# Half of the low parts of two weight streams on GpSimd, and eleven single-pass weight units made three-pass

## The chip, the cores and the metric

The kernel runs on one core of a Trainium2 chip. A core has TensorE (matrix products, PE in the profile; PEld is its weight load), VectorE (DVE), ScalarE (ACT), GpSimd (POOL) and SyncE (SP, which here issues the DMAs). Each engine works through its own list of instructions in order. The metric is the device time of one execution in microseconds (us), and a time for a kernel is a median over runs. A change of about 0.2% (some 5.7 us) is the least that a measurement of this kernel can tell from none.

## The reference, cut to what matters

The network has two layers. Each layer mixes 256 context and 512 latent tokens of width 1024 through four branches, merges the branches, applies one output projection, then a post-norm (layer norm of a scaled residual plus the projection) and a gated MLP with a down projection and a second post-norm:

```
        out_lat = merge(px[0], (ret[1], mla[1], lru[1], ssd[1]))      # ... acc @ w_out
        new_lat = post_norm(h_lat, mod_x[2] * o_lat, ln1_w[l], ln1_b[l])
        f_lat = conv_ffn(modulate(new_lat, mod_x[3], mod_x[4]), ffn_w_up[l], ffn_conv_w[l], ffn_conv_b[l], ffn_w_down[l])
        new_lat = post_norm(new_lat, mod_x[5] * f_lat, ln2_w[l], ln2_b[l])
...
def conv_ffn(h, w_up, conv_w, conv_b, w_down):
    u = centred_conv(h @ w_up, conv_w, conv_b)
    g, v = u[..., :D_FF], u[..., D_FF:]
    return (jax.nn.silu(g) * v) @ w_down
```

The change touches `acc @ w_out` (1024 x 1024) and `(...) @ w_down` (2816 x 1024).

## The kernel before, in words

**Split products.** Most products are made of three matmuls in a 32-bit format of reduced precision (fp32r). An operand x is split into a high part, x rounded to fp32r, and a low part, x minus the high part. The product is then high x high + low x high + high x low, summed in PSUM. `split` (L215 to 217) does this for activations: a cast on ScalarE (L216) and a subtraction on VectorE (`tt`, L143). `unit` (L201 to 213) does it for a weight unit of 128 x 1024: a DMA into a raw tile `wr` (L198, on SP), a cast into `wh` on ScalarE (L205), and two subtractions of 128 x 512 into `wl` on VectorE (called at L209, shown at the helper's line L143). There are three raw tiles (`N_WR`), five high and five low ones.

**Plain products.** `PLAIN` (L55) names units of the output projection that are not split: for those `plain_unit` only loads the raw weights, `plain_pair` hands on the unsplit activations, and `prod` (L513 to 523) issues one fp32 matmul at L519, which the hardware runs as two passes, each with a record of its own. Eleven units are plain: all eight of the context pair in layer 0, and units 3, 5 and 7 of the second latent pair in layer 1.

**The two projections.** The tokens stand in pairs of 128-token tiles: pair 0 is context, pairs 1 and 2 are latents. The output projection works pair by pair in the order 1, 2, 0 (layer 1: 1, 2 alone), with 8 units per pair; the down projection does the same with 22 units per pair. For a unit `tm_wide` (L508) multiplies the pair's two tiles with both halves of the unit: 4 products of 512 columns, into four PSUM tiles `g`. `pair_of` splits the pair's activations for the unit (tiles `t`).

**Post-norm.** After each pair VectorE reads the four PSUM tiles (`o<-g`), adds the residual, takes statistics (`st`, `mv`, `rs`), and GpSimd raises `rs` to the power -1/2 (`rpow`, L190). In the output projection this is done twice. ScalarE normalises (L421), TensorE transposes the pair (L400), and ScalarE and VectorE write the pair into the transposed input `hT2` of the MLP as high and low parts (`hh`, `hl`). The first MLP units (`begin_up`, matmuls at L1518 to 1520) follow the last pair in program order; in layer 0 they need `hT2` of pairs 1 and 2, in layer 1 of pair 1 first.

**Order.** The program is written once; a scheduler of the language turns it into one list per engine by its own costs and by priorities (`tc.high_priority`: weight units and splits ahead of most other work). Those lists are fixed in the program, and an instruction waits for its inputs and buffers in its place in the list. The DMA issues of SP are in one list as well.

Of the kernel before, what the change touches and what calls it, by code (L numbers as in the profile page):

```python
# [8 lines left out]
F32 = mybir.dt.float32  # L9
# [15 lines left out]
NF = D_FF // P  # L25
# [26 lines left out]

N_EARLY = (6, 6)

PLAIN = {(0, 0): (0, 1, 2, 3, 4, 5, 6, 7), (1, 2): (3, 5, 7)}  # L55

STAG = ((0, 2), (0, 0), (3, 5))

# [40 lines left out]
def trunk(tc, xin, cc, const, pv, pr, rows, ada_b, ada_w, w_in, w_uq, w_ukv, w_lg, w_br, w_out, w_up, w_dn, out):  # L99
# [3 lines left out]
    def nm(p):  # L103
        uid[0] += 1
        return f"{p}{uid[0]}"
# [3 lines left out]
    with ExitStack() as ctx:  # L109
# [12 lines left out]
        act, dve, pool, pe, sy = nc.scalar, nc.vector, nc.gpsimd, nc.tensor, nc.sync  # L122
# [4 lines left out]
        def G():  # L127
            return pg.tile([P, 512], F32, tag="g", name=nm("g"))
# [7 lines left out]
        def T256(dt=F32, tag="t"):  # L136
            return tp.tile([P, 256], dt, tag=tag, name=nm("t"), bufs=N_T if tag == "t" else N_V)
# [4 lines left out]
        def tt(o, a, b, op):  # L142
            dve.tensor_tensor(out=o, in0=a, in1=b, op=op)  # L143
# [10 lines left out]
        MUL, ADD, SUB, MAX, MIN = ALU.mult, ALU.add, ALU.subtract, ALU.max, ALU.min  # L154
# [38 lines left out]
        def W4(tag, n, dt=F32R):  # L193
            return wp.tile([P, 1024], dt, tag=tag, name=nm(tag), bufs=n)

        def whole(ap, f=1024, tag="wr"):
            t = W4(tag, {"wr": N_WR, "wh": N_WH, "wl": N_WL}[tag], F32)
            sy.dma_start(out=t[:, 0:f], in_=ap[:, 0:f])  # L198
            return t

        def unit(ap, f=1024, shape=None):  # L201
            with tc.high_priority(offset=O_UNIT):
                raw = whole(ap, f)
                hi = W4("wh", N_WH)
                act.copy(hi[:, 0:f], raw[:, 0:f])  # L205
                lo = W4("wl", N_WL)
                for c in range(0, f, 512):
                    e = min(f, c + 512)
                    tt(lo[:, c:e], raw[:, c:e], hi[:, c:e].bitcast(F32), SUB)  # L209
            if shape is None:  # L210
                return hi, lo
            a, b = shape
            return (hi[:, 0:f].rearrange("p (a b) -> p a b", a=a), lo[:, 0:f].rearrange("p (a b) -> p a b", a=a))

        def split(src, hi, lo):  # L215
            act.copy(hi, src)  # L216
            tt(lo, src, hi.bitcast(F32), SUB)
# [172 lines left out]
        def to_hT(l, which, pair, xh, hT, kps=(0, 1, 2, 3)):  # L390

            strm = 1 if pair == 0 else 0
            t0 = 2 * pair * P
            mc = modc[l]
            for kp in kps:
                ps = C().rearrange("p (k a b) -> p k a b", k=2, a=2)
                for k2 in range(2):
                    k = 2 * kp + k2
                    for a in range(2):
                        pe.transpose(ps[:, k2, a, :], xh[a][k // 4][:, (k % 4) * P:(k % 4 + 1) * P], ident)  # L400
                for k2 in range(2):
                    k = 2 * kp + k2
                    tmp = T256()
                    pk = ps[:, k2, :, :].rearrange("p a b -> p (a b)")
                    if k2:
                        ts(tmp, pk, mc[:, 2 * which + 1, strm, k:k + 1], MUL, mc[:, 2 * which, strm, k:k + 1], ADD)
                    else:
                        act.activation(out=tmp, in_=pk, func=AF.Identity, bias=mc[:, 2 * which, strm, k:k + 1], scale=mc[:, 2 * which + 1, strm, k:k + 1])
                    split(tmp, hT[k][0][:, t0:t0 + 256], hT[k][1][:, t0:t0 + 256])
# [15 lines left out]
        def load_gate(l, which, s):  # L425

            bc = {}
            for h in range(2):
                bc["g", s, h] = S(w=512)
                sy.dma_start(out=bc["g", s, h], in_=modr[l][which, s, h:h + 1, :].to_broadcast([P, 512]))  # L430
            return bc
# [11 lines left out]
        def load_res(pair, res):  # L443

            rs = {}
            for a in range(2):
                for h in range(2):
                    r = rs[a, h] = S(w=512)
                    sy.dma_start(out=r, in_=res[2 * pair + a][:, 512 * h:512 * (h + 1)])
            return rs  # L450
# [44 lines left out]
        def pair_of(t, p, spare=False):  # L495

            with tc.high_priority(offset=100):
                if spare:
                    hi, lo = (hp.tile([P, T], F32R, tag="h", name=nm("h"))[:, 0:256] for _ in range(2))
                else:  # L500
                    hi, lo = T256(F32R, "v"), T256(F32R, "v")
                split(t[:, 2 * p * P:(2 * p + 2) * P], hi, lo)
            return [(hi[:, a * P:(a + 1) * P], lo[:, a * P:(a + 1) * P]) for a in range(2)]

        def plain_pair(t, p):
            return [(t[:, (2 * p + a) * P:(2 * p + a + 1) * P], None) for a in range(2)]

        def plain_unit(ap):  # L508
            with tc.high_priority(offset=100):
                return whole(ap), None  # L510

        def tm_wide(units, nk, xsl, last=0):

            ps = [[G(), G()] for _ in range(2)]

            def prod(k, wh, wl, x, a, h):
                xh, xl = x[a]
                cs = slice(512 * h, 512 * (h + 1))
                pe.matmul(ps[a][h], lhsT=xh, rhs=wh[:, cs], start=k == 0, stop=wl is None and k == nk - 1)  # L519
                if wl is None:  # L520
                    return
                pe.matmul(ps[a][h], lhsT=xl, rhs=wh[:, cs], start=False, stop=False)  # L522
                pe.matmul(ps[a][h], lhsT=xh, rhs=wl[:, cs], start=False, stop=k == nk - 1)  # L523

            held = []
            for k in range(nk):
                held.append((k, *units(k), xsl(k)))
                if k < nk - last:
                    for a in range(2):
                        for h in range(2):  # L530
                            prod(*held[0], a, h)
                    held.clear()
            for a in range(2):
                for h in range(2):
                    for i in held:
                        prod(*i, a, h)
            return ps
# [912 lines left out]
        for l in range(DEPTH):  # L1450
            full = l < DEPTH - 1
            pairs = (1, 2, 0) if full else (1, 2)
# [12 lines left out]
            acc = []  # L1465
# [56 lines left out]
            def begin_up():  # L1522

                for u in range(N_EARLY[l]):
                    ps = early[u] = G() if u < 4 else C()
                    up_part(u, ps, 0, CTX, SEQ if full else 256, True)

            for p in pairs:
                if p == 0:
                    bc.update(load_gate(l, 0, 1))  # L1530
                for a in range(2):
                    mid[2 * p + a] = dp.tile([P, D], F32, name=nm("mid"))
                rs = load_res(p, res)
                plain = PLAIN.get((l, p), ())
                ps = tm_wide(lambda k: plain_unit(w_out[l, k]) if k in plain else unit(w_out[l, k]), 8, lambda k: plain_pair(acc[k], p) if k in plain else pair_of(acc[k], p), STAG[0][l])
                xs = post_norm(p, ps, rs, bc, mid, True, PW[0][l])
                if p == pairs[-1]:
                    begin_up()
                with tc.high_priority(offset=LATER[1]):
                    to_hT(l, 1, p, xs, hT2)  # L1540
# [5 lines left out]
            sv = [None] * NF  # L1546
# [39 lines left out]
            for p in pairs:  # L1586
                if p == 0:
                    bc.update(load_gate(l, 1, 1))
                for a in range(2):
                    t = 2 * p + a  # L1590
                    new[t] = dp.tile([P, D], F32, name=nm("new")) if full else out[(t - 2) * P:(t - 1) * P, :]

                rs = load_res(p, mid)
                ps = tm_wide(lambda k: unit(w_dn[l, k]), NF, lambda k: pair_of(sv[k], p, not full and p == pairs[-1]), STAG[1 if p != pairs[-1] else 2][l])
                xs = post_norm(p, ps, rs, bc, new, full, PW[1 + (p == pairs[-1])][l])
                if full:
                    with tc.high_priority(offset=-LATER[0]):
                        to_hT(l + 1, 0, p, xs, hT)
# [158 lines left out]
```

## Time and profile before

| | us |
|---|---|
| median of 3 runs (lowest, highest) | 2859.02 (2856.67, 2859.52) |
| the profiled execution, and its span | 2861.12, 2859.3 |
| PE busy, of the span | 2801.5 (98%) |
| DVE busy | 1873.3 (66%) |
| ACT busy | 1246.2 (44%) |
| POOL busy | 54.0 (2%) |

Busy shares are averages over the span. A matmul record is longer than the distance to the next one, since matmuls are pipelined: what a matmul costs is read from one start to the next. The same holds for VectorE, where a 128 x 512 instruction is recorded with 0.68 us and the next one starts 0.60 us later. A bracket at a row's end gives the idle time before the instruction and what ended it.

### The profile page before, as it was taken

What the parts mean: (1) busy time and instruction counts of PE and PEld (TensorE: products, weight loads), DVE (VectorE), ACT (ScalarE), POOL (GpSimd) and SP (SyncE); (2) the same over time, 40 slices, a digit from 0 to 9 for tenths busy, and PEclk for the clock granted to TensorE, in tenths of its full rate; (3) what the DMA queues carried; (4) which work ended last, traced back from release to release, by engine and by line L of the source; (5) the groups of instructions that cost most, each with busy time, mean ns of one, the idle gap of its engine ahead of it and who ended that gap; (6) DMA issues with size and microseconds to landing.
All of it is one profiled execution on the core that took longest, in us unless ns stands there. A gap on an engine that the chain in (4) does not pass through costs nothing.

```text
span 2859.3 us, 40144 instructions
## 1 busy us (share of the span) xinstructions
PE 2801.5 (98%) x15248; PEld 2362.5 (83%) x15248; DVE 1873.3 (66%) x3933; ACT 1246.2 (44%) x2231; POOL 54.0 (2%) x70
## 2 busy tenths in 40 slices
PE   7999999999999999999999999999999999899998
PEld 5988879888888886888888778888888888688887
DVE  6454438767566448855557886545887785876667
ACT  4323235434455325533335653244554673453353
POOL 0000000000000001000000000000000000000000
PEclk9999999999999999999999999999999999999999
DMA  6212441445343345311125563121134234542265
GB/s 256 69 49 89 168 155 38 149 169 192 120 169 119 105 155 193 131 65 61 66 85 198 185 203 114 50 98 60 46 112 136 103 114 152 190 152 96 96 201 175
DMA packets 129170, 363.65 MB, mean 127 GB/s; under 512 B 14369, under 2 KB 29601, under 8 KB 128977
## 3 DMA queue, kind: packets, MB, share of 16 engines
q1 hardware_dynamic: 128976, 361.09, 37.0%
q8 instruction: 120, 1.97, 0.3%
q14 instruction: 74, 0.60, 0.1%
HBM read 332.59 MB, written 26.35 MB: 126 GB/s over the span
## 4 chain that ended last, share of the span: by engine, by line
PE 83%; DVE 8%; DMA 4%; ACT 2%; issue 1%; POOL 1%; SPq 0%; POOLq 0%; DVEq 0%; ACTq 0%
PE g L220 18%; PE g L221 18%; PE g L222 18%; PE g L519 3%; PE g L522 3%; PE g L523 3%; PE g L282 2%; PE g L283 2%; PE g L284 2%; DVE wl L143 2%; DVE o L143 1%; DMA wr<-in_w_dn_dram 1%; PE g L349 1%; DVE st L382 1%; PE g L252 1%
## 5 line engine op out<-in xcount | busy, mean ns | idle before, releaser
L143 DVE TENSOR_TENSOR wl<-wr,wh 128x512 fp32r<-128x512 f32 (+1 forms) x866 | 567.0, 682 | 436.1 <-ACT wh L205 402.0
L220 PE MATMUL g<-hh,wh 128*128 128x512 f32 (+1 forms) x2384 | 842.4, 353 | 0.8 <-DVE s L152 0.8
L221 PE MATMUL g<-hl,wh 128*128 128x512 f32 (+1 forms) x2384 | 837.5, 351 | 0.0
L222 PE MATMUL g<-hh,wl 128*128 128x512 f32 (+1 forms) x2384 | 837.0, 351 | 0.0
L205 ACT CAST wh<-wr 128x1024 fp32r<-128x1024 f32 x405 | 423.0, 1046 | 517.9 <-PE g L221 300.6
L220 PEld LDWEIGHTS g<-hh,wh 128*128 128x128 f32 x2384 | 451.2, 189 | 66.2 <-issue 6.6
L222 PEld LDWEIGHTS g<-hh,wl 128*128 128x128 f32 x2384 | 450.8, 189 | 58.5
L221 PEld LDWEIGHTS g<-hl,wh 128*128 128x128 f32 x2384 | 451.2, 189 | 57.4
L143 DVE TENSOR_TENSOR s<-s,s 128x256 f32<-128x256 f32 (+4 forms) x332 | 207.0, 645 | 26.3 <-ACT s L1121 14.6
L519 PE MATMUL g<-wh,t 128*128 128x512 f32 x468 | 184.2, 396 | 3.1 <-ACT t L216 2.5
L522 PE MATMUL g<-wh,t 128*128 128x512 f32 x468 | 183.1, 393 | 1.4 <-DVE t L143 1.3
L523 PE MATMUL g<-wl,t 128*128 128x512 f32 x468 | 182.2, 392 | 0.7 <-DVE wl L143 0.3
L221 PE MATMUL g<-s,wh 128*128 128x512 f32 (+1 forms) x452 | 160.6, 355 | 0.0
L220 PE MATMUL g<-s,wh 128*128 128x512 f32 (+1 forms) x452 | 160.2, 354 | 0.0
L222 PE MATMUL g<-s,wl 128*128 128x512 f32 (+1 forms) x452 | 159.8, 354 | 0.0
L152 DVE SCALAR_TENSOR_TENSOR s<-g,pv,s 128x511 f32<-128x511 f32 (+2 forms) x176 | 111.7, 643 | 61.3 <-ACT s L543 59.4
L152 DVE SCALAR_TENSOR_TENSOR s<-s,s 128x512 f32<-128x512 f32 (+2 forms) x130 | 98.2, 756 | 54.8 <-ACT s L1568 27.4
L152 DVE SCALAR_TENSOR_TENSOR s<-s,g 128x512 f32<-128x512 f32 x118 | 70.7, 604 | 90.8 <-PE g L222 57.3
L282 PE MATMUL g<-wh,hh 128*128 128x512 f32 (+1 forms) x320 | 124.5, 390 | 1.0 <-ACT s L662 1.0
L283 PE MATMUL g<-wh,hl 128*128 128x512 f32 (+1 forms) x320 | 124.3, 388 | 0.0
L284 PE MATMUL g<-wl,hh 128*128 128x512 f32 (+1 forms) x320 | 123.4, 386 | 0.0
L152 DVE SCALAR_TENSOR_TENSOR s<-g,fcg,s 128x511 f32<-128x511 f32 (+1 forms) x128 | 83.9, 655 | 52.0 <-ACT s L543 50.1
(297 smaller groups left out, 4357.9 us busy)
## 6 DMA issues: line engine op xcount, KB each, us to landing
wr<-in_w_in_dram SPq DMA_DIRECT2D x120, 512.0 KB, 3.5
wr<-in_w_dn_dram SPq DMA_DIRECT2D x110, 512.0 KB, 4.3
wr<-in_w_up_dram SPq DMA_DIRECT2D x100, 512.0 KB, 3.5
wh<-in_ada_w_dram SPq DMA_DIRECT2D x46, 512.0 KB, 3.6
wl<-in_ada_w_dram SPq DMA_DIRECT2D x46, 512.0 KB, 5.6
wr<-in_w_out_dram SPq DMA_DIRECT2D x40, 512.0 KB, 3.5
wr<-in_w_br_dram SPq DMA_DIRECT2D x32, 512.0 KB, 3.5
wr<-in_w_in_dram SPq DMA_DIRECT2D x48, 256.0 KB, 3.0
```

The lines of the kernel that those rows point to most:

```text
L143: dve.tensor_tensor(out=o, in0=a, in1=b, op=op)
L152: dve.scalar_tensor_tensor(out=o, in0=a, scalar=s, in1=b, op0=op0, op1=op1)
L205: act.copy(hi[:, 0:f], raw[:, 0:f])
L220: pe.matmul(o, lhsT=sh, rhs=mh, start=start, stop=False)
L221: pe.matmul(o, lhsT=sh, rhs=ml, start=False, stop=False)
L222: pe.matmul(o, lhsT=sl, rhs=mh, start=False, stop=stop)
L282: pe.matmul(o[:, 0:w], lhsT=sh, rhs=wkh, start=k == 0, stop=False)
L283: pe.matmul(o[:, 0:w], lhsT=sl, rhs=wkh, start=False, stop=False)
L284: pe.matmul(o[:, 0:w], lhsT=sh, rhs=wkl, start=False, stop=k == len(ws) - 1)
L519: pe.matmul(ps[a][h], lhsT=xh, rhs=wh[:, cs], start=k == 0, stop=wl is None and k == nk - 1)
L522: pe.matmul(ps[a][h], lhsT=xl, rhs=wh[:, cs], start=False, stop=False)
L523: pe.matmul(ps[a][h], lhsT=xh, rhs=wl[:, cs], start=False, stop=k == nk - 1)
```

## The change

`PLAIN` is empty, so all units of the output projection go through `unit` and all their activations through `pair_of`. And `unit` has a flag with which the second half of a unit's low part is subtracted on GpSimd instead of VectorE; it is set for all units of the output and the down projection (40 and 110 units). The first half stays on VectorE. Other units are made as before.

```diff
-PLAIN = {(0, 0): (0, 1, 2, 3, 4, 5, 6, 7), (1, 2): (3, 5, 7)}
+PLAIN = {}
...
-        def unit(ap, f=1024, shape=None):
+        def unit(ap, f=1024, shape=None, shared=False):
...
                 for c in range(0, f, 512):
                     e = min(f, c + 512)
-                    tt(lo[:, c:e], raw[:, c:e], hi[:, c:e].bitcast(F32), SUB)
+                    eng = pool if shared and c else dve
+                    eng.tensor_tensor(out=lo[:, c:e], in0=raw[:, c:e], in1=hi[:, c:e].bitcast(F32), op=SUB)
...
-                ps = tm_wide(lambda k: plain_unit(w_out[l, k]) if k in plain else unit(w_out[l, k]), 8, lambda k: plain_pair(acc[k], p) if k in plain else pair_of(acc[k], p), STAG[0][l])
+                ps = tm_wide(lambda k: plain_unit(w_out[l, k]) if k in plain else unit(w_out[l, k], shared=True), 8, lambda k: plain_pair(acc[k], p) if k in plain else pair_of(acc[k], p), STAG[0][l])
...
-                ps = tm_wide(lambda k: unit(w_dn[l, k]), NF, lambda k: pair_of(sv[k], p, not full and p == pairs[-1]), STAG[1 if p != pairs[-1] else 2][l])
+                ps = tm_wide(lambda k: unit(w_dn[l, k], shared=True), NF, lambda k: pair_of(sv[k], p, not full and p == pairs[-1]), STAG[1 if p != pairs[-1] else 2][l])
```

The lists of all engines are as before up to the output projection of layer 0, and are ordered anew from there. In the lists below the names end in numbers of the program; `L210` is the subtraction of the changed `unit`, and a line of the changed kernel after it is one higher than before (`BN_STATS` L383 for L382, `MATMUL` L520, L523, L524 for L519, L522, L523).

GpSimd in the output projection of layer 0, changed kernel: `wl` are second halves of units 4 to 7 of pair 2 and then 0 to 2 of pair 0, `rs` the four powers of the post-norm of pair 1.

```order
L210 TENSOR_TENSOR wl_10477<-wr_10473,wh_10475 128x512
L190 TENSOR_TENSOR rs_10254<-rs_10254,nhalf 128x1
L210 TENSOR_TENSOR wl_10500<-wr_10496,wh_10498 128x512
L190 TENSOR_TENSOR rs_10268<-rs_10268,nhalf 128x1
L210 TENSOR_TENSOR wl_10523<-wr_10519,wh_10521 128x512
L210 TENSOR_TENSOR wl_10546<-wr_10542,wh_10544 128x512
L190 TENSOR_TENSOR rs_10288<-rs_10288,nhalf 128x1
L210 TENSOR_TENSOR wl_10715<-wr_10711,wh_10713 128x512
L210 TENSOR_TENSOR wl_10738<-wr_10734,wh_10736 128x512
L190 TENSOR_TENSOR rs_10308<-rs_10308,nhalf 128x1
L210 TENSOR_TENSOR wl_10761<-wr_10757,wh_10759 128x512
```

Before, GpSimd's list holds nothing there but the `rs`; now each stands behind one or two weight halves, which wait for their own DMA and cast.

VectorE in the post-norm of pair 2 (while TensorE works on pair 0), before:

```order
L152 SCALAR_TENSOR_TENSOR nb_10583<-mv_10578,rs_10580 128x1
L382 BN_STATS st_10589<-o_10569 128x6
L382 BN_STATS st_10589<-o_10571 128x6
L143 TENSOR_TENSOR o_10565<-o_10565,s_10017 128x512
L384 BN_AGGR mv_10592<-st_10589 128x2
L143 TENSOR_TENSOR o_10567<-o_10567,s_10019 128x512
L147 TENSOR_SCALAR rs_10594<-mv_10592 128x1
L143 TENSOR_TENSOR o_10565<-o_10565,s_10021 128x512
L152 SCALAR_TENSOR_TENSOR nb_10597<-mv_10592,rs_10594 128x1
```

and in the changed kernel between the same two `nb`:

```order
L152 SCALAR_TENSOR_TENSOR nb_10583<-mv_10578,rs_10580 128x1
L383 BN_STATS st_10589<-o_10569 128x6
L383 BN_STATS st_10589<-o_10571 128x6
L210 TENSOR_TENSOR wl_10807<-wr_10803,wh_10805 128x512
L385 BN_AGGR mv_10592<-st_10589 128x2
L143 TENSOR_TENSOR o_10565<-o_10565,s_10017 128x512
L147 TENSOR_SCALAR rs_10594<-mv_10592 128x1
L143 TENSOR_TENSOR o_10567<-o_10567,s_10019 128x512
L143 TENSOR_TENSOR t_10834<-s_9816,t_10833 128x256
L152 SCALAR_TENSOR_TENSOR nb_10597<-mv_10592,rs_10594 128x1
```

The post-norm's own instructions stand in the same order; a weight half and an activation's low part of pair 0 have come between them.

TensorE at the end of pair 0, before:

```order
L400 MATMUL c_10680<-cst,s_10628 128x128
L400 MATMUL c_10680<-cst,s_10608 128x128
L400 MATMUL c_10680<-cst,s_10628 128x128
L519 MATMUL g_10710<-wr_10741,s_9816 128x512
L519 MATMUL g_10707<-wr_10747,s_9914 128x512
L519 MATMUL g_10708<-wr_10747,s_9914 128x512
L519 MATMUL g_10709<-wr_10747,s_9914 128x512
L519 MATMUL g_10710<-wr_10747,s_9914 128x512
L519 MATMUL g_10707<-wr_10753,s_10005 128x512
L519 MATMUL g_10708<-wr_10753,s_10005 128x512
L519 MATMUL g_10709<-wr_10753,s_10005 128x512
L519 MATMUL g_10710<-wr_10753,s_10005 128x512
```

and in the changed kernel:

```order
L401 MATMUL c_10667<-cst,s_10628 128x128
L401 MATMUL c_10667<-cst,s_10608 128x128
L401 MATMUL c_10667<-cst,s_10628 128x128
L401 MATMUL c_10680<-cst,s_10628 128x128
L401 MATMUL c_10680<-cst,s_10608 128x128
L401 MATMUL c_10680<-cst,s_10628 128x128
L1519 MATMUL g_10971<-hh_10025,wh_10974 128x512
L1520 MATMUL g_10971<-hl_10026,wh_10974 128x512
L1521 MATMUL g_10971<-hh_10025,wl_10976 128x512
```

The last transposes of pair 2 stood nine products ahead of the end of pair 0; they now stand behind all of pair 0, and the first MLP unit follows them directly.

## Rows read from the trace of the kernel before

**Rows 1.** the page's busy times, x instructions

```profile
PE 2801.5 (98%) x15248; PEld 2362.5 (83%) x15248; DVE 1873.3 (66%) x3933; ACT 1246.2 (44%) x2231; POOL 54.0 (2%) x70
```

**Rows 2.** timeline of TensorE: start, us, line, out<-in, records

```profile
1096.47 16.47 PE L519 MATMUL g<-wr,s 128*128 128x512 f32 x38
1126.61 0.79 PE L1518 MATMUL g<-hh,wh 128*128 128x512 f32 x1
...
2461.90 0.39 PE L519 MATMUL g<-wh,t 128*128 128x512 f32 x1
2462.58 0.39 PE L519 MATMUL g<-wh,t 128*128 128x512 f32 x1
```

**Rows 3.** two stretches of layer 0: us, busy PE, PEld, DVE, ACT, POOL

```profile
1069.50:1093.20 23.70, 23.04 (x102) 17.86 (x100) 22.68 (x51) 11.01 (x17) 2.73 (x4) 1.00 0.38 135
1068.70:1123.80 55.10, 52.12 (x190) 32.12 (x189) 48.40 (x112) 27.92 (x51) 5.89 (x8) 1.00 0.56 191
```

**Rows 4.** VectorE's groups, 1068.7 to 1123.8: busy us, mean ns, idle before

```profile
L143 DVE TENSOR_TENSOR o<-o,s 128x512 f32<-128x512 f32 x16 | 10.7, 674 | 0.0
L143 DVE TENSOR_TENSOR wl<-wr,wh 128x512 fp32r<-128x512 f32 x10 | 6.6, 674 | 0.0
L143 DVE TENSOR_TENSOR hl<-t,hh 128x256 fp32r<-128x256 f32 x16 | 6.3, 415 | 0.0
L152 DVE SCALAR_TENSOR_TENSOR o<-s,o 128x512 f32<-128x512 f32 x8 | 5.3, 670 | 0.5 <-DMA s<-in_xin_dram 0.5
L149 DVE TENSOR_SCALAR t<-c,modc 128x256 f32<-128x256 f32 x8 | 4.3, 540 | 2.7 <-ACT t L408 2.6
L152 DVE SCALAR_TENSOR_TENSOR nb<-mv,rs 128x1 f32<-128x1 f32 x8 | 1.3, 160 | 3.2 <-POOL rs L190 3.0
```

**Rows 5.** timeline of VectorE, layer 0's output projection

```profile
1070.75 0.41 DVE L143 TENSOR_TENSOR t<-s,t 128x256 fp32r<-128x256 f32 x1
1071.08 1.28 DVE L152 SCALAR_TENSOR_TENSOR o<-s,o 128x512 f32<-128x512 f32 x2
1072.29 0.68 DVE L143 TENSOR_TENSOR wl<-wr,wh 128x512 fp32r<-128x512 f32 x1
...
1122.71 1.08 DVE L143 TENSOR_TENSOR hl<-t,hh 128x256 fp32r<-128x256 f32 x3
```

**Rows 6.** timeline of VectorE and GpSimd around two powers

```profile
1092.53 0.68 DVE L143 TENSOR_TENSOR o<-g,s 128x512 f32<-128x512 f32 x1
1092.76 0.55 POOL L190 TENSOR_TENSOR rs<-rs,nhalf 128x1 f32<-128x1 f32 x1 [5.02 <-DVE rs L147]
...
1104.48 0.68 DVE L152 SCALAR_TENSOR_TENSOR o<-s,o 128x512 f32<-128x512 f32 x1
1104.73 0.84 POOL L190 TENSOR_TENSOR rs<-rs,nhalf 128x1 f32<-128x1 f32 x1 [11.42 <-DVE rs L147]
```

**Rows 7.** GpSimd's groups: the widest power

```profile
L190 POOL TENSOR_TENSOR ss<-ss,nhalf 128x12 f32<-128x12 f32 x2 | 4.5, 2268 | 82.0 <-DVE ss L149 82.0
```

**Rows 8.** layer 1's output projection: TensorE's and VectorE's timeline

```profile
2479.31 0.68 PE L1518 MATMUL g<-hh,wh 128*128 128x256 f32 x1
2480.06 0.42 DVE L143 TENSOR_TENSOR hl<-t,hh 128x256 fp32r<-128x256 f32 x1
2493.71 0.58 PE L1520 MATMUL g<-hh,wl 128*128 128x256 f32 x1 [2.18 <-DVE wl L143]
```

**Rows 9.** layer 0's down projection: stretch, and VectorE's group in it

```profile
1570.00:1690.00 120.00, 113.27 (x493) 87.76 (x493) 97.70 (x225) 72.61 (x122) 5.01 (x7) 1.00 0.63 210
L143 DVE TENSOR_TENSOR wl<-wr,wh 128x512 fp32r<-128x512 f32 x80 | 52.6, 684 | 17.0 <-ACT wh L205 16.9
```

**Rows 10.** layer 1's down projection, steady part: timelines; DMA issues

```profile
2754.18 1.30 DVE L143 TENSOR_TENSOR wl<-wr,wh 128x512 fp32r<-128x512 f32 x2 [0.53 <-ACT wh L205]
2753.09 1.05 ACT L205 CAST wh<-wr 128x1024 fp32r<-128x1024 f32 x1
wr<-in_w_dn_dram SPq DMA_DIRECT2D x22, 512.0 KB, 4.4
```

## The prediction

> **What bounds the kernel now.** I read the page's busy times first, then the idle time of TensorE, then the engines' busy times stretch by stretch. TensorE is busy for 2801.5 of 2859.3 us [rows 1], so outside a few places any product that gets shorter shortens the run. The places where it does not are those in which another engine is late, and the change acts on just these: the output projection, where VectorE is busy for 22.68 of 23.70 us while pair 2 is multiplied, and for 48.40 of 55.10 us from the start of pair 1's post-norm to the last low part of pair 2 [rows 3]. There VectorE sets when `hT2` is ready, and TensorE is given enough products to reach the first MLP unit at 1126.61 [rows 2], when the last low parts (1122.71 and 1.08 us) had just been written [rows 5]. The engine on the chain and the engine that is full are two here, and nearly level.
>
> **TensorE's part.** 38 plain passes take 16.47 us; less the 0.59 us by which the last record outlasts its start, that is 0.429 us for a pass and 0.858 for a product of two. A split product takes 0.68 us from one start to the same matmul of the next product [rows 2]. So each of the 44 plain products (8 units of 4 in layer 0, 3 of 4 in layer 1) gets 0.175 us shorter: 5.6 us in layer 0, 2.1 in layer 1, 7.7 in all, if nothing else ends later.
>
> **What is added and moved.** ScalarE gets 11 casts of 1.05 us [rows 10] and 11 casts of activations. Eight of each, some 12 us, come into a stretch in which it is busy for 27.92 of 55.10 us [rows 3], so they are covered. Bytes and DMA issues stay as they are. A raw tile is now free when GpSimd has read it. In the steady part a raw tile goes through a cast of 1.05, two halves of 1.30 together and a DMA of 4.4 us [rows 10], 6.75 us in all, and comes round every three units of 12 matmuls, 3 x 12 x 0.227 = 8.2 us: 1.4 us are spare. VectorE loses 139 second halves and gains 11 first halves and 11 low parts of activations. One instruction of 512 columns takes 0.60 us of it, one of 256 takes 0.33 (start to start) [rows 5].
>
> **What a half costs on GpSimd.** No such instruction is in the trace. A power over 1 column takes 0.55 us undisturbed [rows 6] and over 12 columns 2.27 [rows 7], so 0.156 us a column and 0.39 fixed. A power per column is another operation, and at that price 512 columns would take 80 us and the run many milliseconds; I give that end to a rival below. The other end is VectorE's 0.68 us for the same subtraction [rows 5]. The nearest row is that one; with GpSimd's fixed 0.39 us I take 1.1 us. The Trainium skill, "GPSIMD Engine Reference", section "Performance versus the Vector engine", gives 4497 ns for a two-input sum of 2048 columns; scaled, that is an estimate of 1.1 to 1.2 us, and the sum would stay. No run here shows it.
>
> **What a half on GpSimd costs VectorE.** The same power takes 0.55 us beside a VectorE instruction with one operand in PSUM and one in SBUF (`o<-g,s`), but 0.84 us beside one with both operands in SBUF (`o<-s,o`) [rows 6]. So GpSimd is held until VectorE's two-operand read ends: the two share something. The reverse, VectorE held by a long GpSimd read, cannot be seen with one column. Its bounds are 0 and the whole 1.1 us for each half. In the full stretch 28.9 us of groups with two SBUF operands and 7 x 0.41 us of `t` make 31.8 of 48.4 us, 66% [rows 3 to 5]. I take 66% of 1.1, so 0.73 us for each half where VectorE is full, since the row that shows the conflict is the only one that bears on it. That is more than the 0.60 us that the half saved. The Trainium skill, "SBUF — State Buffer", section "Who interferes with whom", says that a VectorE instruction with two SBUF inputs and a GpSimd one that reads SBUF exclude each other, and that whichever starts first keeps the other out for its whole length. The trace agrees for one direction (0.55 against 0.84 us). By that rule 0.73 stands; without it the sum falls to the first rival's.
>
> **Layer 0's output projection.** In VectorE's list from the first eviction of pair 1 to the last low part of pair 2 stand 16 weight halves where there were 10, 15 `t` where there were 7, and 12 evictions where there were 8: 6 x 0.60 + 8 x 0.33 + 4 x 0.60 = 8.6 us more. (The halves of pair 2 moved away are in that count; pair 0's are what comes in.) Twelve GpSimd halves run beside it: 12 x 0.73 = 8.8 us. VectorE's 6.4 us of waits there (0.5, 2.7, 3.2) [rows 4] take in half of their length, 3.2. So the last low part lands 14.2 us later, at 1138.0 instead of 1123.8. The first MLP unit may begin 7 x 0.68 = 4.8 us earlier, since it takes eight steps, at 1133.2: 6.6 us later than before. TensorE's 5.6 us turn into waiting at the transposes and at this unit. Low end: nothing is blocked and all waits absorb, last part at 1126.0, first unit not before the products and the exposed step from the transposes to the first low part, about -4. High end: every half blocks 1.1 us and nothing absorbs, 8.6 + 13.2 - 4.8 later than 1123.8, +14.2.
>
> **Layer 1's output projection.** The same, smaller: three halves, three `t`, one eviction and one residual addition more before the last low part of pair 1 (4.0 us), and five GpSimd halves (3.7). Before, that part ended at 2480.48, while the first unit (start 2479.31) needs it 7 x 0.36 = 2.5 us after its start, so 1.3 us were spare [rows 8]: +6.4 at the first unit. The wait of 2.18 us for an MLP low part soon after [rows 8] then goes, since the parts have had that time: +4. Bounds -2.1 (only the products count) and +8.
>
> **Layer 0's down projection.** From 1570 to 1690 VectorE is busy for 97.7 of 120 us and TensorE idle for 6.7 [rows 9]. Forty of its 80 weight halves leave, -24 us; forty halves on GpSimd block VectorE while it is busy, at most 40 x 0.73 = 29. The load stays about as it was, but each `rs` now waits behind a weight half in GpSimd's list, and `nb` and all behind it on VectorE wait for `rs`. I take +2, with bounds -6.7 (all of TensorE's idle time goes) and +10 (seven `rs` late by a half and a wait each).
>
> **Elsewhere.** In layer 1's down projection a unit would ask 0.60 + 0.33 + 1.1 us of VectorE and GpSimd in turn, against 2.7 us of TensorE: nothing shows. The end, after the last matmul, has no weight halves.
>
> **Sum.** +6.6 + 4 + 2 = +12.6 on the profiled execution's 2861.1 us gives 2873.7; that execution is 2.1 us above the median of the runs, so 2871.6, say 2872. All low ends together give 2859.0 - 12.8 = 2846, all high ends +32, 2891.
>
> **Rivals.**
> *GpSimd works beside VectorE* (the faster side). If a long GpSimd read does not hold VectorE up, layer 0 comes to about -3, layer 1 to -2, the down projection to -4: 2850. For it: VectorE's instructions beside the powers keep their 0.68 us [rows 6]; against it: those powers read one column.
> *The extra order eats the saving.* If each half costs VectorE some 0.3 us, the first unit of layer 0 starts 8.6 + 3.6 - 3.2 - 4.8 = 4.2 us after 1123.8, 1.4 later than before, layer 1 stays, the down projection gives 2 back: 2858 to 2860. For it: the waits [rows 4] are as long as the blocking would be.
> *GpSimd is too slow for three raw tiles.* From 1.3 + 1.4 = 2.7 us for a half with its waits, the ring of raw tiles sets the pace of 150 units: at 3.3 us, (3.3 - 2.7) / 3 x 150 = 30 us on top of the blocking, 2890 and beyond. For it: the slow powers; against it: a subtraction needs no series.
>
> **Chances.** My forecast 0.45 (its own range 2864 to 2882), the first rival 0.22, the second 0.20, the third 0.13. What this measurement can tell from no change is 0.2%, 5.7 us. Of the first rival 0.18 lies below that, the second fills the middle, and nearly all the rest lies above: faster 0.19, same 0.20, slower 0.61. The range 2847 to 2890 leaves out part of the first and of the third.
>
> **What would show it.** Right: `wl` on GpSimd near 1.1 us, longer when VectorE reads two operands; VectorE records in these stretches longer than 0.68 us or waiting on nothing but GpSimd's read; the first L1519 of layer 0 later than 1126.6 after a wait on VectorE or ScalarE; no plain passes, and 132 more split matmuls at 0.227. Wrong: that first unit at 1121 to 1124, VectorE's records unchanged beside GpSimd's, or a GpSimd half over 2.7 us with waits of ScalarE on the DMA of raw tiles throughout.

## The result, and the profile after

The changed kernel takes 2894.77 us (median of 4 runs, 2894.00 to 2897.38), the kernel before 2858.23 beside it: a ratio of 1.0128, 95% interval 1.0115 to 1.0140, so 36.5 us slower. Forecast were 12.6 us slower, with 2890 us as the upper end: the direction was right, the size was a third of what came.

The busy times of the page after, which answer to [rows 1], and two of its groups (line, engine, operation, tiles, shapes, count | busy us, mean ns | idle before, and what ended most of it):

```profile
PE 2808.4 (97%) x15292; PEld 2377.3 (82%) x15292; DVE 1879.0 (65%) x3816; ACT 1259.7 (44%) x2253; POOL 305.4 (11%) x220
L210 DVE TENSOR_TENSOR wl<-wr,wh 128x512 fp32r<-128x512 f32 x682 | 479.7, 724 | 400.0 <-ACT wh L205 394.2
L210 POOL TENSOR_TENSOR wl<-wr,wh 128x512 fp32r<-128x512 f32 x150 | 248.6, 1661 | 1245.1 <-ACT wh L205 1240.0
```

VectorE executes 117 instructions fewer than before and is busy 5.7 us longer. A GpSimd half lasts 1.66 us in the mean.

Where the time went is read from one milestone of TensorE's timeline to the next. Lengths are in us, all from the profiled executions (span 2859.3 before, 2893.2 after):

| stretch | before | after | difference | forecast |
|---|---|---|---|---|
| layer 0 output projection, to the first MLP unit | 78.8 | 92.5 | +13.7 | +6.6 |
| first MLP unit to the first up unit behind the early ones | 36.7 | 39.4 | +2.7 | none |
| layer 0 down projection | 195.6 | 206.1 | +10.5 | +2 |
| layer 1 output projection and early units | 97.9 | 105.1 | +7.2 | +4 |
| layer 1 down projection | 120.1 | 122.7 | +2.6 | 0 |
| all else | 2330.2 | 2327.4 | -2.8 | 0 |

TensorE's timeline at the first MLP unit after, the answer to [rows 2] (1126.61 there):

```profile
1132.27 1.58 PE L401 MATMUL c<-cst,s 128*128 128x128 f32 x12 [0.39 <-ACT s L422]
1138.99 0.76 PE L1519 MATMUL g<-hh,wh 128*128 128x512 f32 x1 [5.14 <-DVE o L143]
1139.55 0.63 PE L1520 MATMUL g<-hl,wh 128*128 128x512 f32 x1
1139.98 0.63 PE L1521 MATMUL g<-hh,wl 128*128 128x512 f32 x1
...
1144.27 0.40 PE L1520 MATMUL g<-hl,wh 128*128 128x512 f32 x1
1144.50 0.40 PE L1521 MATMUL g<-hh,wl 128*128 128x512 f32 x1
```

The first unit waits 5.14 us for an eviction `o` of VectorE, and its first products are 0.43 us apart, later 0.23. The windows of the same trace (us, busy of PE, PEld, DVE, ACT, POOL, then the granted clock, DMA share, GB/s) show why:

```profile
1046.50:1139.00 92.50, 76.16 (x323) 58.18 (x321) 76.43 (x137) 50.75 (x82) 39.39 (x28) 0.95 0.57 186
1137.00:1139.00 2.00, 0.01 (x1) 0.04 (x1) 0.85 (x2) 1.68 (x3) 0.00 (x0) 0.50 1.04 384
1140.00:1143.00 3.00, 3.00 (x9) 2.32 (x8) 3.00 (x8) 1.06 (x3) 0.00 (x0) 0.50 0.09 34
1145.00:1148.00 3.00, 3.00 (x15) 2.47 (x14) 3.00 (x8) 0.29 (x1) 0.00 (x0) 1.00 0.54 175
1512.70:1718.80 206.10, 192.04 (x827) 152.28 (x826) 146.22 (x267) 111.86 (x181) 107.42 (x70) 0.98 0.58 195
```

While TensorE waited the granted clock fell to 0.50 (the level of 1.2 GHz); it stood there while the first products ran, and at 1.00 again in the window from 1145.00. So this wait cost more than its length. Not every wait does: after 2.38 us without a product, from 1176.03 on, the clock still stood at 1.00. With the trace cut into steps of 0.1 us, those in which TensorE is busy at the lower level lose 18.8 us over the run, against 9.0 before.

VectorE and GpSimd in the layer 0 down projection after, around the post-norm of pair 1; the answer to [rows 6]:

```profile
1568.98 0.69 DVE L210 TENSOR_TENSOR wl<-wr,wh 128x512 fp32r<-128x512 f32 x1 [0.53 <-ACT wh L205]
1569.03 1.80 POOL L210 TENSOR_TENSOR wl<-wr,wh 128x512 fp32r<-128x512 f32 x1 [0.92 <-ACT wh L205]
...
1571.75 1.30 POOL L210 TENSOR_TENSOR wl<-wr,wh 128x512 fp32r<-128x512 f32 x1 [0.92 <-ACT wh L205]
1571.83 1.77 DVE L210 TENSOR_TENSOR wl<-wr,wh 128x512 fp32r<-128x512 f32 x1
1573.52 1.87 DVE L143 TENSOR_TENSOR o<-g,s 128x512 f32<-128x512 f32 x3
1574.46 1.30 POOL L210 TENSOR_TENSOR wl<-wr,wh 128x512 fp32r<-128x512 f32 x1 [1.41 <-ACT wh L205]
1575.32 0.73 DVE L143 TENSOR_TENSOR t<-s,t 128x256 fp32r<-128x256 f32 x1
...
1580.69 0.93 POOL L190 TENSOR_TENSOR rs<-rs,nhalf 128x1 f32<-128x1 f32 x1 [1.36 <-DVE rs L147]
1581.60 1.28 POOL L210 TENSOR_TENSOR wl<-wr,wh 128x512 fp32r<-128x512 f32 x1
1581.66 1.24 DVE L152 SCALAR_TENSOR_TENSOR nb<-mv,rs 128x1 f32<-128x1 f32 x1
```

The reader sees the exclusion both ways. At 1568.98 VectorE is first, and GpSimd's half ends 0.5 us late. At 1571.75 GpSimd is first: VectorE's half, which begins 0.08 us later, lasts 1.77 instead of 0.68 us. The three evictions `o<-g,s`, with one operand in PSUM, keep their 0.6 us each, though the last of them begins inside the half of 1574.46, and the `t` behind them is held until 1575.8, when that half ends. The last three rows are the costliest form: the end of `rs` lets `nb` go on VectorE and the next half on GpSimd, GpSimd is 0.06 us ahead, and an instruction of one column takes 1.24 us instead of 0.16. Of 32 `nb` 12 are held in this way, and behind each stand ScalarE's normalisation and the transposes.

### The profile page after: what moved, and what is told of

Same layout as the page of the kernel before. It is cut to its first block, busy times and chain, and to the rows that moved or that the text cites. A ratio compares the mean times of both kernels' runs of the same rounds, so it can differ in the third digit from the quotient of the medians.

```text
span 2893.2 us, 40616 instructions
## 1 busy us (share of the span) xinstructions
PE 2808.4 (97%) x15292; PEld 2377.3 (82%) x15292; DVE 1879.0 (65%) x3816; ACT 1259.7 (44%) x2253; POOL 305.4 (11%) x220
## 4 chain that ended last, share of the span: by engine, by line
PE 83%; DVE 7%; DMA 3%; ACT 2%; issue 2%; POOL 2%; SPq 0%; POOLq 0%; DVEq 0%; ACTq 0%
PE g L221 18%; PE g L222 18%; PE g L223 18%; PE g L523 3%; PE g L520 3%; PE g L524 3%; PE g L283 2%; PE g L284 2%; PE g L285 2%; PE g L350 1%; POOL wl L210 1%; DVE wl L210 1%; PE g L253 1%; PE g L252 1%; PE g L251 1%
## 5 line engine op out<-in xcount | busy, mean ns | idle before, releaser
L210 DVE TENSOR_TENSOR wl<-wr,wh 128x512 fp32r<-128x512 f32 x682 | 479.7, 724 | 400.0 <-ACT wh L205 394.2
L205 ACT CAST wh<-wr 128x1024 fp32r<-128x1024 f32 x416 | 434.2, 1046 | 504.8 <-PE g L222 306.6
L210 POOL TENSOR_TENSOR wl<-wr,wh 128x512 fp32r<-128x512 f32 x150 | 248.6, 1661 | 1245.1 <-ACT wh L205 1240.0
L523 PE MATMUL g<-wh,t 128*128 128x512 f32 x512 | 204.9, 401 | 11.3 <-DVE t L143 10.5
L520 PE MATMUL g<-wh,t 128*128 128x512 f32 x512 | 202.3, 399 | 5.8 <-ACT t L217 3.7
L524 PE MATMUL g<-wl,t 128*128 128x512 f32 x512 | 202.2, 397 | 2.1 <-DVE wl L210 2.1
L523 PEld LDWEIGHTS g<-wh,t 128*128 128x128 f32 x512 | 97.6, 191 | 39.9 <-DVE t L143 20.8
```

The lines of the kernel that those rows point to most:

```text
L210: eng.tensor_tensor(out=lo[:, c:e], in0=raw[:, c:e], in1=hi[:, c:e].bitcast(F32), op=SUB)
```

## The experiments

My theory is the hold: a GpSimd half that reads SBUF and a VectorE instruction with two SBUF operands shut each other out, and on the chains of the post-norms that is what costs. (Such an instruction is called held below.) The rivals are order (the extra splits and the reordered lists cost) and latency (the half just comes later). All ratios are against the kernel before on the same chip. Stretches are those of the table above, the first two of them added; "down" is layer 0's.

| run | ratio (95%) | layer 0 out + early | down | layer 1 out + early |
|---|---|---|---|---|
| before | 1 | 115.5 | 195.6 | 97.9 |
| changed | 1.0128 (1.0115 to 1.0140) | 131.9 | 206.1 | 105.1 |
| split alone | 1.0059 (1.0045 to 1.0072) | 128.0 | 193.5 | 101.1 |
| halves alone | 1.0074 (1.0061 to 1.0086) | 120.8 | 205.2 | 103.0 |
| halves, down alone | 1.0047 (1.0034 to 1.0059) | 117.2 | 204.2 | 98.3 |
| changed, write only | 0.9980 (0.9971 to 0.9989) | 121.8 | 188.2 | 94.0 |
| changed, 32 columns | 0.9991 (0.9983 to 1.0000) | 121.9 | 189.0 | 94.2 |
| changed, copy | 1.0012 (1.0003 to 1.0021) | 123.8 | 193.1 | 97.0 |
| changed, gate tiles | 1.0106 (1.0092 to 1.0120) | 127.2 | 205.5 | 104.9 |
| split alone, gate tiles | 1.0046 (1.0033 to 1.0059) | 123.8 | 193.7 | 101.4 |
| 32 columns, gate tiles | 0.9974 (0.9964 to 0.9983) | 116.9 | 189.0 | 94.5 |
| down, beside post-norms | 1.0029 (1.0018 to 1.0041) | 114.9 | 202.7 | 96.9 |
| down, the rest | 1.0010 (1.0002 to 1.0019) | 117.0 | 198.4 | 96.5 |
| changed, 256 columns | 1.0058 (1.0044 to 1.0071) | 125.8 | 196.3 | 103.2 |

**The two parts of the change.** The first run splits all units and leaves all low parts on VectorE; against the changed kernel:

```diff
-... unit(w_out[l, k], shared=True) ... unit(w_dn[l, k], shared=True)
+... unit(w_out[l, k]) ... unit(w_dn[l, k])
```

> The changed kernel with all low parts on VectorE again (PLAIN stays empty): the splitting alone. Exclusion theory (a GpSimd half that reads SBUF and a VectorE instruction with two SBUF operands shut each other out for their whole length): the layer 0 output projection still suffers, since 18 second halves of 0.60 us come back to VectorE where 12 blocked stretches go; the down projections are as before, and the 33.9 us of the spans fall to about 15: 2868 to 2876. Order rival (the extra splits and the reordered lists make the time, GpSimd hardly matters): 2885 to 2895. Latency rival (a GpSimd half just arrives later): no GpSimd, so little is left, 2858 to 2865.

Measured 2875.70 us, 1.0059, within the range of the theory and of neither rival. The other way round, with `PLAIN` as before:

```diff
-PLAIN = {}
+PLAIN = {(0, 0): (0, 1, 2, 3, 4, 5, 6, 7), (1, 2): (3, 5, 7)}
```

> The kernel before (the eleven units stay plain) with second halves on GpSimd in both projections: the halves without the splitting. Exclusion theory: the down stages as measured with them alone (+13.4 us by the ratio), and in the output projections 29 GpSimd halves (no plain unit has one) hold VectorE: +3 to +8 more, so ratio 1.0058 to 1.0075, some 2877 to 2882. Order rival (splitting is what costs in the output projection): nothing more than the down stages, ratio 1.0047, 2874.

Measured 2881.27 us, 1.0074. Both parts cost, and they add up: 1.0059 and 1.0074 together are 1.0133, against 1.0128. With `PLAIN` as before and the flag for `w_dn` alone:

> The kernel before with second halves on GpSimd in the down projection alone; PLAIN as before, output projection as before. Exclusion theory: the two down stages grow as in the changed kernel, by 10.5 and 2.6 us, so 2871 (2867 to 2875). Order rival: no unit is split anew, 2856 to 2860. Latency rival: also 2865 to 2871, but then TensorE waits for low parts written by GpSimd and not for VectorE.

Measured 2872.15 us, 1.0047. TensorE's waits in the down projection of layer 0 (us in total, times, longest), first of that run, then of the kernel before:

```profile
PE c L401 <- ACT s L422: 5.8, 3, 2.8
PE g L523 <- DVE t L143: 4.0, 6, 1.7
PE g L520 <- ACT t L217: 1.2, 1, 1.2
PE g L520 <- DVE o L143: 0.3, 1, 0.3
```

```profile
PE c L400 <- ACT s L421: 2.5, 3, 1.0
PE g L519 <- ACT t L216: 2.5, 2, 2.0
PE g L519 <- ACT wh L205: 0.6, 1, 0.6
PE g L522 <- DVE t L143: 0.5, 2, 0.3
PE g L523 <- DVE wl L143: 0.3, 1, 0.3
```

No wait is for a low part from GpSimd, and in the whole trace of the changed kernel none of TensorE's is, so latency falls. What grew are the waits for the normalised rows `s`, which stand behind `nb`, and for `t`: just the chains with held instructions. In the changed kernel ScalarE's waits for `nb` before it writes `s` are 10.8 us there, against 3.2 before.

**The hold itself.** Three kernels in which the lists of VectorE, ScalarE and SP are instruction for instruction those of the changed kernel (TensorE's too, but for a few products in other order in the second); only what GpSimd does for a half differs. Each leaves something out: the first fills the second half of the low part with zeros, the second keeps 32 of its columns, the third puts the raw columns in its place.

```diff
-                    eng.tensor_tensor(out=lo[:, c:e], in0=raw[:, c:e], in1=hi[:, c:e].bitcast(F32), op=SUB)
+                    if shared and c:
+                        pool.memset(lo[:, c:e].bitcast(F32), 0.0)
```

> The changed kernel, but GpSimd fills the second half of the low part with zeros (512 columns written, nothing read), so the second half's correction is left out of the product. The lists of the other engines are the same as in the changed kernel. Exclusion theory: without GpSimd's read nothing is held, VectorE's t, nb and wl keep 0.41, 0.16 and 0.68 us, and the time falls to 2850 to 2862. Order rival: 2885 to 2895, as the lists are the same. Latency rival: 2850 to 2862 too, since a fill waits for no cast; the next run tells these two apart.

Measured 2854.61 us, 0.9980. Two groups, VectorE's `t` and GpSimd's fill:

```profile
L143 DVE TENSOR_TENSOR t<-s,t 128x256 fp32r<-128x256 f32 x128 | 53.9, 422 | 66.6 <-ACT t L220 66.3
L210 POOL MEMSET wl<- 128x512 f32 x150 | 78.7, 527 | 1352.8 <-PE g L226 1115.0 <-PE g L527 219.0 <-issue 11.6
```

```diff
+                        pool.tensor_tensor(out=lo[:, c:c + 32], in0=raw[:, c:c + 32], in1=hi[:, c:c + 32].bitcast(F32), op=SUB)
...
+                pe.matmul(..., rhs=wl[:, 32 * h:32 * h + 512], ...)
```

> The changed kernel, but GpSimd subtracts 32 of the 512 columns, with the same two SBUF reads, the same waits and the same place in its list; the other 480 columns of the second half are left out (the low product of the second half takes a shifted window of what is there). Exclusion theory: the hold is as long as the instruction, so a GpSimd record of 0.3 us or less instead of 1.26 takes three quarters of the blocking away: 2852 to 2866. Order rival: 2885 to 2895. Latency rival by the wait for cast and DMA in GpSimd's list: 2885 to 2892, since those waits stay.

Measured 2857.63 us, 0.9991. Its busy times, and GpSimd's group:

```profile
PE 2791.8 (98%) x15292; PEld 2371.2 (83%) x15292; DVE 1805.7 (63%) x3816; ACT 1259.7 (44%) x2253; POOL 152.7 (5%) x220
L210 POOL TENSOR_TENSOR wl<-wr,wh 128x32 fp32r<-128x32 f32 x150 | 95.6, 637 | 1359.6 <-ACT wh L205 1340.7 <-DMA s<-in_rows_dram 7.4 <-PE g L527 5.0
```

With the same 3816 instructions VectorE is busy 1805.7 us instead of 1879.0: 73.3 us of held time hung on the length of GpSimd's reads alone. For these the order rival falls, since the lists are the same and the time is lower by 1.0128 - 0.9991, some 39 us. The splitting alone still costs its 1.0059, with no half on GpSimd at all; a part of that follows below.

```diff
+                        pool.tensor_copy(out=lo[:, c:e], in_=raw[:, c:e])
```

> The changed kernel, but GpSimd copies the 512 raw columns into the second half of the low part (one SBUF operand instead of two), so the second low half is wrong by that and only the time is read. The other engines' lists are those of the changed kernel. Exclusion by any SBUF read: VectorE's two-operand records are held for as long as the copy runs, and its busy time with the same 3816 instructions lies above the 1805.7 us of the short half in proportion: a copy of 0.5 us would give some 1815 us and 2860 to 2866, one of 1.25 us 1879 and 2890 to 2895. Exclusion only between two two-operand instructions: no hold, VectorE at 1803 to 1806 us, 2854 to 2860, and no VectorE record longer than its own length.

Measured 2864.36 us, 1.0012, VectorE 1837.7 us busy. Its rows at one unit:

```profile
1561.38 0.62 POOL L210 CAST wl<-wr 128x512 fp32r<-128x512 f32 x1 [2.10 <-PE g L527]
1561.50 0.77 DVE L143 TENSOR_TENSOR t<-s,t 128x256 fp32r<-128x256 f32 x1 [1.01 <-ACT t L220]
```

`t` is held from its 0.43 to 0.77 us, so one SBUF operand on GpSimd is enough. The Trainium skill, "SBUF — State Buffer", section "Who interferes with whom", names a GpSimd instruction that reads SBUF, and not one that only writes it; the copy (0.77 us) and the fill (0.43 at most) agree. The copy waits for no cast and so falls on other instructions than the subtraction does; the sizes of the two are not to be compared.

**A second cost, in SP's list.** Before and after, SP's timeline (start, us, line, tiles, records) at the loads of pair 0's gate, and after it VectorE's eviction that needs them:

```profile
1114.45 0.32 SPq L471 DMA_DIRECT2D mid<-o  x1
1114.82 0.96 SPq L430 DMA_DIRECT2D s<-modr  x2
```

```profile
1127.36 3.79 SPq L198 DMA_DIRECT2D wr<-in_w_up_dram  x3
1131.20 1.48 SPq L431 DMA_DIRECT2D s<-modr  x2
1138.15 0.69 DVE L143 TENSOR_TENSOR o<-g,s 128x512 f32<-128x512 f32 x1 [1.95 <-DMA s<-modr]
```

The splitting moved these loads behind raw tiles of MLP units, which wait for VectorE; with the splitting alone they are late too, at 1125.48. The eviction, and with it the PSUM tile of the first MLP unit, waits for them. The edit gives the gate two tiles of its own (the room for them comes from a tile `dt` placed in one of them):

```diff
+            own = [cur[-1].tile([P, 512], F32, tag="gate", name=nm("own"), bufs=2) for h in range(2)]
...
+                    gates["g", 1, h] = own[h]
+                    sy.dma_start(out=own[h], in_=modr[l][0, 1, h:h + 1, :].to_broadcast([P, 512]))
...
-                    bc.update(load_gate(l, 0, 1))
+                    bc.update(gates)
```

> The changed kernel with two tiles of their own for pair 0's gate (modr), so that its two loads are issued early in layer 0 instead of behind four raw tiles of MLP units, where SP issued them at 1131.20. Theory that the splitting has a second cost beside the hold, this load (TensorE's first MLP unit waits for the first eviction of pair 0, and that for the load): the first unit starts 2 to 4 us earlier after the start of the projection than 92.5 us, ratio to before 1.0115 to 1.012. Rival (the hold alone decides; hl of pair 2 would be as late): 92 to 93 us, ratio 1.0128.

Measured 2891.55 us, 1.0106, a little more gain than expected; the first unit starts after 89.6 us instead of 92.5, the first up unit after 127.2 instead of 131.9.

> The split-only kernel (all low parts on VectorE, PLAIN empty) with the same two tiles for the gate. Second-cost theory: its first MLP unit, 86.0 us after the start of the projection with the gate behind the raw tiles, starts 2 to 5 us earlier, and the ratio falls from 1.0059 to 1.0040 to 1.0052. Rival (VectorE's added low parts alone decide): 85 to 86 us, ratio 1.0059.

Measured 2875.30 us, 1.0046: the first unit after 85.7 us (not the 2 to 5 us earlier that I expected), the first up unit after 123.8 instead of 128.0. By the ratio alone, whose interval reaches 1.0059, that is unclear; the intervals of the other two pairs overlap or touch as well.

> The changed kernel with GpSimd subtracting 32 of its 512 columns (the other 480 are left out of the low product) and with the two tiles for pair 0's gate: no long hold and no late gate. If these two are all that the change costs, what stays is the gain of shorter products and less VectorE work: the layer 0 output projection to the first up unit falls from 121.9 to 116 to 119 us (before 115.5), and the ratio from 0.9991 to 0.9970 to 0.9980. If the gate costs nothing once the hold is gone: 0.9991.

Measured 2851.94 us, 0.9974, the first up unit after 116.9 us instead of 121.9. Three pairs of kernels, each read in one trace, agree on 4 to 5 us in this stretch, and the wait on the eviction (5.1, 3.1 and 5.4 us) is gone from it. Not all of it is won: in its place TensorE waits longer for `s` at the last transposes (3.4 us at once in the changed kernel with gate tiles), so that its idle time falls by 3.1, 1.4 and 4.7 us. In the first two pairs the clock gives back another 2.4 and 2.6 us. The edit also reorders parts of the lists of VectorE, ScalarE and SP, so the load is not shown to be all of it. Without long hold and late gate the kernel is some 7 us faster than before; it leaves out most of the second halves, so it is no version to use.

**Where a hold costs.** The halves of the down projection in two groups:

```diff
-... unit(w_dn[l, k], shared=True)
+... unit(w_dn[l, k], shared=p != pairs[0] and k < 15)
```

> The kernel before with GpSimd halves in the down projection alone, and there only for units 0 to 14 of every pair but the first: those that run beside the post-norm of the pair before (30 units in layer 0, 15 in layer 1, of the 110). Chain theory (a held instruction costs time where VectorE is on the chain from the products to the next pair's transposes and t): nearly all of the 13.4 us that the 110 units cost, ratio 1.0035 to 1.0050. Load theory (each held microsecond costs alike, wherever it falls): 45 of 110 halves, 5.5 us, ratio 1.0019.

Measured 2867.13 us, 1.0029. And with `p == pairs[0] or k >= 15`:

> The other 65 units of the 110: all units of the first pair, and units 15 to 21 of the others, with their second halves on GpSimd; the rest as in the kernel before. Chain theory: VectorE is on no chain there, ratio 0.9995 to 1.0010. Load theory: 65 of 110 halves, 7.9 us, ratio 1.0028.

Measured 2861.90 us, 1.0010. So 45 halves beside post-norms cost 8.3 us, 0.18 each, and the other 65 cost 2.9, 0.04 each. The load theory falls by the second run (1.0028 lies outside its interval; the 1.0019 for the first is just inside). In layer 0's stretch the 30 units of the first group cost 7.1 us and the other 36 cost 2.8. The chain theory expected more of the first run, and the two together are 2 us short of the 13.4 for all 110, which is within their intervals.

**Half the length.**

```diff
-                for c in range(0, f, 512):
+                for c, e in ((0, 768), (768, 1024)) if shared else ...:
```

> The changed kernel with 256 columns of each low part on GpSimd instead of 512, and the other 768 on VectorE in one instruction. Between 32 columns (0.25 us undisturbed) and 512 (1.255) a straight line gives 0.72 us for 256. Exclusion theory with a price by length: 57% of the 40 us that the hold costs (23), and half of the 19.5 us between split-only and no hold lost again, from -2.6: 7 + 23 = 30 us, ratio 1.0105 (1.008 to 1.0115). Price by number of holds, whatever their length: 1.0128 or more.

Measured 2875.38 us, 1.0058: a miss, 13 us less than a price by length gave. The shortest record was 0.72 us as worked out, but the kernel takes no longer than with all low parts on VectorE (1.0059). The down projection takes 196.3 us, against 195.6 before. Perhaps a hold of that length fits into what VectorE waits anyway; no run shows it, and VectorE's own part of a unit differs here as well (768 columns in one instruction). How the price goes with the length stays open.

## Why the prediction fell short

**Right, in part by luck.** A plain product's replacement, the exclusion as such, its direction, and the size of the hold where I worked it out: 0.73 us for each half in the full stretch. In the layer 0 output projection VectorE was busy for 76.43 us after, and for 62.75 with 32 columns and the same 137 instructions. The windows of that run, there and in layer 0's down projection, and of the kernel before in the down projection:

```profile
1046.00:1128.20 82.20, 71.83 (x323) 56.46 (x322) 62.75 (x137) 50.67 (x82) 16.78 (x28) 0.98 0.63 210
1502.20:1691.20 189.00, 186.55 (x826) 150.51 (x825) 117.51 (x267) 111.44 (x181) 45.83 (x70) 1.00 0.65 212
```

```profile
1498.30:1693.90 195.60, 188.87 (x827) 149.98 (x826) 151.41 (x329) 112.36 (x181) 5.85 (x8) 1.00 0.62 205
```

That is 13.7 us over 20 halves (28 GpSimd records less 8 `rs`), 0.68 each. The two factors were off and made up for each other: GpSimd's half, forecast at 1.1 us, takes 1.255 at least, and 0.68 is 54% of that, not 66%. From the first eviction of pair 1 to the last low part of pair 2, where I had counted 12 halves, lie 13.

**Where the steps failed.** The spans differ by 33.9 us against 12.6 forecast. Of the 21.3 us between them 9.8 lie in layer 0's output projection with the units behind it, 8.5 in layer 0's down projection, 3.2 in layer 1's output projection and 2.6 in layer 1's down projection; all else gave 2.8 back. Even all my high ends together, 2891 us, fall short of the result.

**The step that failed in the down projection of layer 0: "The load stays about as it was", so +2.** The load did: VectorE was busy for 146.2 us of the stretch after and for 151.4 before, since 62 instructions left it, and 146.22 - 117.51 = 28.7 us of hold came, 0.46 for each half. But equal load is not equal time. VectorE was idle for 44 us of the stretch before, so what left it freed little; the holds beside the post-norms fell on `nb`, `t` and `o`, behind which TensorE waits. Without the long hold the stretch takes 189.0 us, 6.6 less than before (my low end was -6.7), with it 206.1: the hold is worth 17 us there, and I had netted it against a saving in another place. The path that I had named for the +2, `rs` behind a weight half, is not where it came from: VectorE's waits for `rs` are 3.0 us after and 2.7 before.

**The step that failed in layer 0's output projection: "The first MLP unit may begin 4.8 us earlier", set by the last low part.** What releases it after is another: an eviction behind a load that SP issues 16 us later than before. I had written that DMA issues stay as they are, and did not follow SP's list. By the table's runs the 16.4 us here are 10.0 of hold (131.9 - 121.9), 5.0 of the late gate (121.9 - 116.9) and 1.4 of the rest (116.9 - 115.5); my 6.6 were 8.8 of hold, nothing for the gate and -2.2 for the rest (1123.8 + 8.6 - 3.2 - 4.8, against 1126.6). So the hold was near, and the gate at nothing is the largest miss.

**Not in the sum at all: the clock.** Behind three of the longer waits in layer 0 (2.71, 5.14 and 2.90 us) TensorE's products run at 0.50 for some us. Over the run 9.8 us more than before are lost so; they are part of the stretches above.

**Layer 1** went as worked out but larger: +7.2 against +4, and without the long hold -3.7, below my low end of -2.1, which had only the products in it. Its down projection, forecast at 0, came out 2.6 us longer, 2.1 of it by the hold (120.6 us with 32 columns).

**The rivals.** GpSimd freely beside VectorE was put at 2850; with the hold taken out, and most of the second halves with it, the runs gave 2854.6 and 2857.6, and 2851.9 with the gate mended. The rival of 0.3 us a half, 2858 to 2860, had too little: the halves cost VectorE 0.68 and 0.46. The slow GpSimd forecast a similar total for another reason: the halves stayed under its 2.7 us in the mean, TensorE waited for none of them, and ScalarE's casts waited for raw tiles in the down projection of layer 0 for 12.5 us, against 27.2 before.

## What to carry to other kernels

Work that goes from VectorE to GpSimd must be priced by what VectorE does beside it: a held instruction shows as a longer record (`nb` 1.24 us for 0.16), not as idle time, so compare busy time at equal instruction counts. Price the hold on the chain that the held instruction belongs to; do not net it against busy time saved elsewhere. And when a change reorders the lists, read SP's too: a load that slips behind tiles which wait becomes a wait of TensorE, and a long wait of TensorE can cost clock besides.

## What the runs showed of the hardware

- A subtraction of 128 x 32, 128 x 256 and 128 x 512 takes GpSimd 0.247, 0.717 and 1.255 us where nothing holds it: about 2.1 ns a column and 0.18 us fixed. VectorE's next 512 columns start after 0.60.
- Beside a GpSimd fill of 512 columns (0.527 us, nothing read) `t` stays at 0.427 us or less in all 128 records and `nb` at 0.164 or less in all 32. A copy of 512 columns (0.62 us) holds both: `t` up to 0.88 us, and 11 `nb` at 0.54.
- VectorE instructions with one operand in PSUM are not held: `o<-g,s` has a mean of 681 ns after and 683 before over its 40 records, the longest after is 694, and six begin well inside a half.
- Two SBUF operands on VectorE are not the only form that is held. After the change a copy of 128 x 8 with one (`z<-pv`) lasts 1.28 us instead of 0.17 and ends with GpSimd's half, and one of the TENSOR_SCALAR instructions `s<-s` of 128 x 16 lasts 1.23 instead of 0.17. The statistics `st<-o`, with one SBUF operand too, keep 0.68 us in the mean, and none of 72 is over 0.70.
